# A written head, direct column transposes, and 2048-column modulation products in a hybrid decoder layer

## The chip, the cores and the metric

The kernel runs on one core of one Trainium2 chip. The metric is the device time of one execution in microseconds (us). Three runs of the kernel before took 1594.01, 1604.08 and 1601.12 us, median 1601.12.

## The reference

One layer of a decoder trunk on 256 tokens of width 2048, in float32, batch 1. What bears on this case is its start:

```python
c_act = jax.nn.silu(c)
mod = c_act @ w_mod[l] + b_mod[l]                 # 2048 -> 6 * 2048
sh1, sc1, g1, sh2, sc2, g2 = jnp.split(mod, 6, axis=-1)
h = _rms_norm(x, mix_norm_pre[l]) * (1.0 + sc1[:, None]) + sh1[:, None]
y = _token_mixer(h, ...)                          # begins with proj = h @ w_in
x = x + g1[:, None] * _rms_norm(y, mix_norm_post[l])
h = _rms_norm(x, ffn_norm_pre[l]) * (1.0 + sc2[:, None]) + sh2[:, None]
y = _conv_ffn(h, ...)                             # w_up, causal conv of width 3, silu gate, w_down
x = x + g2[:, None] * _rms_norm(y, ffn_norm_post[l])
```

The token mixer holds a sliding-window attention and a gated linear attention, whose branches are gated, added and projected. All matrices together are some 400 MB, and each is read once.

## The kernel before, in words

Every weight matrix goes through one loop over *parts* of 128x1024 (512 KB). A part is loaded into `raw` (4 buffers), split by ACT into `hi` (a cast to fp32r, L272) and by DVE into `lo` (the rest, L276; 3 buffers each), and used by TensorE three parts later. A product in this precision is three matmuls: hi x hi, lo x hi, hi x lo (L292 to L294).

*Phase 1* multiplies the scaled input by 2048 columns of `w_in` (`wS`), *phase 2* by the 2048 columns of the output gate (`wOG`). Each has 16 *items*, one for each block of 128 input channels. An item is two parts, four column blocks `n`, two token tiles `t`, so 2 x 2 x 2 x 3 = 24 matmuls of 512 columns. All eight PSUM banks accumulate over the 16 items and are emptied at the phase's end (`evac_1`, L379 and L381, and `evac_2`).

The input of item c needs modulation. Its column of `mod` is not a matmul: 128 rows of `w_mod` transposed (`wM[idx]`, 128x2048) lie on the partitions, and DVE multiplies them by `cact`, a copy of silu(c) on every partition, and sums along the row (L207). Before, this is done in two halves of 1024 columns, each in one of four buffers (`early`), and a small instruction adds both sums and the bias (L211, `modc`). In phase 1 another makes the scale `acol` (L355), then ACT writes `h` hi (L357) and DVE `h` lo (L358) from `xnT`, the transposed normalised input. In phase 2 ACT adds the shift as well (L365), casts (L297), and DVE subtracts (L298). A half whose place in the loop is q is multiplied when part q is prepared, and the buffer that it leaves is filled for a later half at once.

The *head* is all that comes before the first phase-1 matmul. It makes `cact`: DVE scales the identity by each of 16 columns of silu(c) (L136, into `t2k`), and TensorE multiplies by a matrix of ones, four matmuls of 512 columns in float32, which show as two records each (L139). ACT copies them out (L143). For each of two token tiles, DVE and ACT each square and sum one half of x (L147, L149), a power on POOL gives the reciprocal root (L115), DVE makes a diagonal of it (L120), and TensorE multiplies 16 blocks of x by that diagonal, which scales and transposes at once (L171; float32, so two records for a block). ACT copies the result to `xnT` (L173, four blocks at a time).

The order of TensorE and of the DMA queue (SP) is the order of the code. DVE and ACT follow the code inside blocks marked as manual, among them the head; elsewhere the scheduler sets their order when the program is built. All loads stand in one queue of SP, which also waits there for the buffer of a load to come free: a load that waits holds back those behind it.

Of the kernel before, what the change touches and what calls it, by code (L numbers as in the profile page):

```python
# [13 lines left out]
ALU = mybir.AluOpType  # L14
# [3 lines left out]
P = 128  # L18
# [20 lines left out]
def block_kernel(ctx: ExitStack, tc: tile.TileContext, x, cvec, pos, idn, cst, vec, vec2, gmask,  # L39
# [82 lines left out]


    cact = region("cact", [P, D], "cact")
    ones = t2k()
    nc.gpsimd.memset(ones, 1.0)
# [3 lines left out]
    with tc.manual_schedule(engines={ET.DVE, ET.Activation}):  # L130
        nc.scalar.activation(ccol, ccol, AF.Silu)

        def c_diag(n):
            dg = t2k()
            for j in range(4):
                nc.vector.tensor_scalar(out=dg[:, j * P:(j + 1) * P], in0=ident, scalar1=ccol[:, 4 * n + j:4 * n + j + 1],  # L136
                                        scalar2=None, op0=ALU.mult)
            ps = bank(n)
            nc.tensor.matmul(out=ps, lhsT=ones[:, :P], rhs=dg, start=True, stop=True)  # L139
            return ps  # L140

        def c_copy(n, ps):
            nc.scalar.copy(cact[:, n * 512:(n + 1) * 512], ps)  # L143

        def sums(t):
            ssx = small(2, "ssx")
            nc.vector.scalar_tensor_tensor(out=junk[:, t, :HW], in0=xh[:, t, :HW], scalar=1.0, in1=xh[:, t, :HW],  # L147
                                           op0=ALU.mult, op1=ALU.mult, accum_out=ssx[:, 0:1])
            nc.scalar.activation(junk[:, t, HW:], xh[:, t, HW:], AF.Square, accum_out=ssx[:, 1:2])  # L149
            return ssx  # L150

        def scale(ssx):
            ssy = small(1, "ssy")
            nc.vector.tensor_tensor(ssy, ssx[:, 0:1], ssx[:, 1:2], op=ALU.add)
            return diag_of(rstd_of(ssy, 1, float(D)))

        cps = [c_diag(n) for n in range(3)]
        c_copy(0, cps[0])
        s0 = sums(0)
        cps.append(c_diag(3))  # L160
        c_copy(1, cps[1])
        c_copy(2, cps[2])
        dgs = [scale(s0)]
        s1 = sums(1)
        c_copy(3, cps[3])
        for t in range(2):
            for q in range(4):
                pt = bank((4, 5, 6, 7, 0, 1, 2, 3)[4 * t + q])
                for j in range(4):
                    c = 4 * q + j  # L170
                    nc.tensor.matmul(out=pt[:, j * P:(j + 1) * P], lhsT=xh[:, t, c * P:(c + 1) * P], rhs=dgs[t],  # L171
                                     start=True, stop=True)
                nc.scalar.copy(xnT[:, 4 * q:4 * q + 4, t * P:(t + 1) * P], pt.rearrange("p (c t) -> p c t", c=4))  # L173
            if t == 0:
                dgs.append(scale(s1))

# [9 lines left out]
    def mod_halves(idx, post=None):  # L186
        it = {}
        return [dict(kind="mod", src=wM[idx], it=it, idx=idx, half=h, post=post) for h in range(2)]

    def bias_halves(c):  # L190
        return [dict(kind="bias", src=wS[c], c=c, half=h) for h in range(2)]
# [108 lines left out]
    def outer_mm(c, n_all, x_of, evac, split=False, mid=None):  # L300


        def one(c, t, n, hi, lo):
            xh_, xl_ = x_of()
            i = 4 * t + n
            if c == 0:
                S["acc", i] = bank(i)
            ns = slice((n % 2) * 512, (n % 2 + 1) * 512)
            ts = slice(t * P, (t + 1) * P)
            mm3(S["acc", i], xh_(c)[:, ts], xl_(c)[:, ts], hi[:, ns], lo[:, ns], c == 0, c == n_all - 1)  # L310
            if c == n_all - 1:
                evac(t, n, S["acc", i])

        def go(it, half, hi, lo):
            if not split or c < n_all - 3:
                for n in (2 * half, 2 * half + 1):
                    for t in range(2):
                        one(c, t, n, hi, lo)
                return
            for n in (2 * half, 2 * half + 1):  # L320
                one(c, 0, n, hi, lo)
            S["held", c, half] = (hi, lo)
            if c == n_all - 1 and half == 1:
# [28 lines left out]
    def make_h1(c):  # L352
        def go():
            a = acol[:, c:c + 1]
            nc.vector.scalar_tensor_tensor(out=a, in0=modc[:, 16 + c:17 + c], scalar=1.0,  # L355
                                           in1=vc[:, V_PRE1 + c:V_PRE1 + c + 1], op0=ALU.add, op1=ALU.mult)
            nc.scalar.activation(h_hi[:, c], xnT[:, c], AF.Copy, scale=a)  # L357
            nc.vector.scalar_tensor_tensor(out=h_lo[:, c], in0=xnT[:, c], scalar=a, in1=h_hi[:, c].bitcast(F32),  # L358
                                           op0=ALU.mult, op1=ALU.subtract)
        return go  # L360
# [11 lines left out]
    def evac_1(t, n, ps):  # L372
        if t == 0 and n == 0:
            S["C"] = region("C", [P, 4096], "qkv")
            S["qkv"] = S["C"][:, 0:3072].rearrange("p (t n) -> p t n", t=2)
            S["vb", 3] = vbp.tile([P, 2, 512], F32, name="vb", tag="vb")
        dst = S["vb", 3][:, t] if n == 3 else S["qkv"][:, t, n * 512:(n + 1) * 512]
        if t == 0:
            nc.scalar.copy(dst, ps)  # L379
        else:  # L380
            nc.vector.tensor_copy(dst, ps)  # L381
# [783 lines left out]
    def aux_step(q):  # L1165

        nonlocal aux_loaded, aux_done
        while aux_done < len(aux) and aux[aux_done]["pos"] <= q:
            aux_proc(aux_done)
            aux_done += 1  # L1170
        while aux_loaded < min(len(aux), aux_done + (4 if aux_done < N_EARLY - 2 else 3 if aux_done < N_PRE - 2 else 2)):
            aux_load(aux_loaded)
            aux_loaded += 1

    for q in range(n + PR):
# [9 lines left out]
        if q < n:  # L1185
# [99 lines left out]
```

## Time and profile before

| | before |
|---|---|
| runs, us | 1594.01, 1601.12, 1604.08 |
| profiled execution, us | 1597.75 |
| its span, first to last instruction, us | 1595.6 |
| TensorE busy | 1563.3 us, 98% of the span |
| VectorE (DVE) busy | 1222.5 us, 77% |
| ScalarE (ACT) busy | 825.7 us, 52% |
| bytes moved | 403.18 MB, mean 253 GB/s |
| mean granted TensorE clock | 0.997 |

The profiled execution stands 2.15 us over its span, and 3.37 us under the median of the runs. Busy time of TensorE is modelled from pipelined matmuls, so 98% says that it hardly ever waits, not that nothing could be quicker. Times within the trace are us from the span's start.

### The profile page before, as it was taken

What the parts mean: (1) busy time and instruction counts of PE and PEld (TensorE: products, weight loads), DVE (VectorE), ACT (ScalarE), POOL (GpSimd) and SP (SyncE); (2) the same over time, 40 slices, a digit from 0 to 9 for tenths busy, and PEclk for the clock granted to TensorE, in tenths of its full rate; (3) what the DMA queues carried; (4) which work ended last, traced back from release to release, by engine and by line L of the source; (5) the groups of instructions that cost most, each with busy time, mean ns of one, the idle gap of its engine ahead of it and who ended that gap; (6) DMA issues with size and microseconds to landing.
All of it is one profiled execution on the core that took longest, in us unless ns stands there. A gap on an engine that the chain in (4) does not pass through costs nothing.

```text
span 1595.6 us, 21287 instructions
## 1 busy us (share of the span) xinstructions
PE 1563.3 (98%) x7752; PEld 1293.2 (81%) x7752; DVE 1222.5 (77%) x1869; ACT 825.7 (52%) x1221; POOL 17.0 (1%) x35
## 2 busy tenths in 40 slices
PE   8999999999999999999999999999999999999997
PEld 6878888877767788777888888888778888888886
DVE  7999989968977778877778877777546777776446
ACT  5455565544477544443366555555335555555333
POOL 0000000000000000000000000000000000000001
PEclk9999999999999999999999999999999999999999
DMA  9999987877777799889935667677665555555554
GB/s 367 382 352 410 360 274 257 277 273 256 250 244 263 257 306 326 293 293 314 354 133 199 230 231 238 217 245 231 231 224 187 182 185 185 186 186 189 194 197 132
DMA packets 154841, 403.18 MB, mean 253 GB/s; under 512 B 12720, under 2 KB 70704, under 8 KB 154480
## 3 DMA queue, kind: packets, MB, share of 16 engines
q1 hardware_dynamic: 154736, 401.82, 72.9%
q8 instruction: 61, 1.00, 0.3%
q14 instruction: 44, 0.36, 0.1%
HBM read 399.68 MB, written 2.10 MB: 252 GB/s over the span
## 4 chain that ended last, share of the span: by engine, by line
PE 31%; DMA 22%; DVE 13%; issue 5%; ACT 2%; SPq 1%; POOL 0%; DVEq 0%; POOLq 0%; ACTq 0%
DMA aux<-in_wM_dram 21%; PE ps L343 16%; DVE lo L276 6%; PE ps L293 5%; PE ps L294 5%; PE ps L292 5%; DVE aux L207 2%; DMA raw<-in_wO_dram 1%; ACT hi L272 1%; SPq L251 0%; DVE aux L348 0%; DVE t2k L742 0%; DVE t2k L1093 0%; DVE y L1134 0%; SPq L253 0%
## 5 line engine op out<-in xcount | busy, mean ns | idle before, releaser
L272 ACT CAST hi<-raw 128x1024 fp32r<-128x1024 f32 x520 | 544.9, 1050 | 476.1 <-PE ps L294 366.9
L276 DVE TENSOR_TENSOR lo<-raw,hi 128x1024 fp32r<-128x1024 f32 x518 | 629.2, 1221 | 142.0 <-ACT hi L272 139.6
L343 PE MATMUL ps<-h,hi 128*128 128x512 f32 x1664 | 582.0, 398 | 1.0 <-DVE h L1051 1.0
L343 PE MATMUL ps<-h,lo 128*128 128x256 f32 x1664 | 451.0, 281 | 1.0 <-DVE lo L276 0.9
L343 PEld LDWEIGHTS ps<-h,hi 128*128 128x128 f32 x1664 | 306.4, 188 | 69.2 <-issue 1.3
L343 PEld LDWEIGHTS ps<-h,lo 128*128 128x128 f32 x1664 | 314.0, 189 | 13.8 <-DVE lo L276 4.4
L207 DVE SCALAR_TENSOR_TENSOR aux<-aux,cact 128x1024 f32<-128x1024 f32 x128 | 156.4, 1223 | 145.7 <-DMA aux<-in_wM_dram 145.6
L292 PE MATMUL ps<-hi,h 128*128 128x512 f32 x608 | 240.0, 395 | 1.6 <-ACT h L297 1.1
L293 PE MATMUL ps<-lo,h 128*128 128x512 f32 x608 | 237.4, 391 | 2.6 <-DVE lo L276 2.5
L294 PE MATMUL ps<-hi,h 128*128 128x512 f32 x608 | 237.1, 390 | 1.5 <-DVE h L298 0.8
L293 PEld LDWEIGHTS ps<-lo,h 128*128 128x128 f32 x608 | 114.2, 188 | 29.2 <-DVE lo L276 4.9
L294 PEld LDWEIGHTS ps<-hi,h 128*128 128x128 f32 x608 | 114.1, 188 | 26.9 <-DVE h L298 1.2
L292 PEld LDWEIGHTS ps<-hi,h 128*128 128x128 f32 x608 | 114.2, 188 | 26.7 <-ACT h L297 1.5
L293 PE MATMUL ps<-lo,act_ab 128*128 128x512 f32 x256 | 100.3, 392 | 2.2 <-DVE lo L276 2.2
L294 PE MATMUL ps<-hi,act_ab 128*128 128x512 f32 x256 | 99.7, 389 | 0.0
L292 PE MATMUL ps<-hi,act_ab 128*128 128x512 f32 x256 | 99.7, 389 | 0.0
L207 DVE SCALAR_TENSOR_TENSOR early<-early,cact 128x1024 f32<-128x1024 f32 x64 | 78.0, 1218 | 1.3 <-ACT cact L143 1.3
L347 ACT ACTIVATE aux<-ps 128x256 f32<-128x256 f32 x88 | 33.5, 380 | 75.4 <-PE ps L343 75.2
L1090 ACT ACTIVATE t2k<-aux,vc 128x256 f32<-128x256 f32 x88 | 52.8, 601 | 26.6 <-DVE aux L348 26.4
L348 DVE SCALAR_TENSOR_TENSOR aux<-ps,aux 128x256 f32<-128x256 f32 x88 | 37.0, 421 | 35.6 <-ACT aux L347 35.6
L293 PEld LDWEIGHTS ps<-lo,act_ab 128*128 128x128 f32 x256 | 48.0, 188 | 14.4 <-DVE lo L276 4.6
L292 PEld LDWEIGHTS ps<-hi,act_ab 128*128 128x128 f32 x256 | 48.0, 188 | 10.1
(270 smaller groups left out, 1614.2 us busy)
## 6 DMA issues: line engine op xcount, KB each, us to landing
raw<-in_wU_dram SPq DMA_DIRECT2D x176, 512.0 KB, 3.8
aux<-in_wM_dram SPq DMA_DIRECT2D x128, 512.0 KB, 6.0
raw<-in_wD_dram SPq DMA_DIRECT2D x88, 512.0 KB, 3.9
early<-in_wM_dram SPq DMA_DIRECT2D x64, 512.0 KB, 6.7
raw<-in_wS_dram SPq DMA_DIRECT2D x32, 512.0 KB, 6.4
raw<-in_wOG_dram SPq DMA_DIRECT2D x32, 512.0 KB, 7.0
aux<-in_wS_dram SPq DMA_DIRECT2D x32, 512.0 KB, 5.7
raw<-in_wQK_dram SPq DMA_DIRECT2D x32, 512.0 KB, 5.4
```

What stands on the lines that cost most here:

```text
L207: nc.vector.scalar_tensor_tensor(out=raw, in0=raw, scalar=1.0, in1=cact[:, half * HW:(half + 1) * HW], op0=ALU.mult, op1=ALU.mult, accum_o ...
L272: nc.scalar.copy(hi[:, :w], raw)
L276: nc.vector.tensor_tensor(lo[:, :w], raw, hi[:, :w].bitcast(F32), op=ALU.subtract)
L292: nc.tensor.matmul(out=o, lhsT=lh, rhs=rh, start=start, stop=False)
L293: nc.tensor.matmul(out=o, lhsT=lh, rhs=rl, start=False, stop=False)
L294: nc.tensor.matmul(out=o, lhsT=ll, rhs=rh, start=False, stop=stop)
L343: nc.tensor.matmul(out=o, lhsT=w, rhs=m, start=c == 0 and o is ps, stop=c == nk - 1 and o is ps)
L347: nc.scalar.activation(o, ps[:, TOK:], AF.Copy, scale=scale)
L348: nc.vector.scalar_tensor_tensor(out=o, in0=ps[:, :TOK], scalar=scale, in1=o, op0=ALU.mult, op1=ALU.add)
L1090: nc.scalar.activation(z, u, AF.Identity, scale=w2, bias=vc2[:, W_CB + f:W_CB + f + 1])
```

## The change

The three small loads (identity, conditioning vector, bias table) leave the SP queue for ACT's queue. The 16 diagonal scalings and the four matmuls with ones give way to 16 transposes, on TensorE, of a column of silu(c) spread over 128 columns; the fill of the ones on POOL goes. Three of the four half-squares go to DVE. For token tile 1 the diagonal goes: DVE scales x itself, in place, and TensorE transposes it in its transpose mode. The order of the head, with the first two parts' casts in it, is written out. A modulation column is one product over 2048 columns (`mod_wide`) when both halves are there; 1 + scale is folded into the bias table once, so that in phase 1 one small instruction gives `acol`. The first four matmul groups of phase 1 are reordered so that all hi x hi come first. At the end of phase 1 ACT empties two banks that DVE emptied before.

```diff
-    nc.sync.dma_start(out=ident, in_=idn)
-    nc.sync.dma_start(out=ccol, in_=cvec)
+    nc.scalar.dma_start(out=ccol, in_=cvec)
+    nc.scalar.dma_start(out=ident, in_=idn)
...
-    nc.sync.dma_start(out=vc, in_=vec)
...
+    nc.scalar.activation(ccol, ccol, AF.Silu)
+    nc.scalar.dma_start(out=vc, in_=vec)
+    for n in range(4):
+        ps = bank((2, 6, 3, 7)[n])
+        for j in range(4):
+            nc.tensor.transpose(ps[:, j * P:(j + 1) * P], ccol[:, 4 * n + j:4 * n + j + 1].to_broadcast([P, P]), ident)
+        cps.append(ps)
...
+    c_copy(0)
+    square_v(0, 0)
+    nc.scalar.activation(junk[:, 0, HW:], xh[:, 0, HW:], AF.Square, accum_out=ssx[0][:, 1:2])
+    for n in range(1, 4):
+        c_copy(n)
+    square_v(1, 0)
+    rs = rstd_x(0)
+    square_v(1, 1)
+    dg0 = diag_of(rs)
+    rs = rstd_x(1)
+    for q in range(2):
+        xs = xh[:, 1, q * HW:(q + 1) * HW]
+        nc.vector.tensor_scalar(out=xs, in0=xs, scalar1=rs, scalar2=None, op0=ALU.mult)
+    bs = vc[:, V_BMOD + 16:V_BMOD + 32]
+    nc.vector.tensor_scalar(out=bs, in0=bs, scalar1=1.0, scalar2=None, op0=ALU.add)
...
+    def mod_wide(a, raw):
+        idx = a["idx"]
+        acc = small(2, "macc")[:, 0:1]
+        nc.vector.scalar_tensor_tensor(out=raw, in0=raw, scalar=1.0, in1=cact, op0=ALU.mult, op1=ALU.mult, accum_out=acc)
+        b = vc[:, V_BMOD + idx:V_BMOD + idx + 1]
+        if idx < 16:
+            nc.vector.tensor_tensor(modc[:, idx:idx + 1], acc, b, op=ALU.add)
+        else:
+            nc.vector.scalar_tensor_tensor(out=acol[:, idx - 16:idx - 15], in0=acc, scalar=b,
+                                           in1=vc[:, V_PRE1 + idx - 16:V_PRE1 + idx - 15], op0=ALU.add, op1=ALU.mult)
+        a["post"]()
...
-        if t == 0:
+        if t == 0 or n < 2:
             nc.scalar.copy(dst, ps)
...
-        while aux_done < len(aux) and aux[aux_done]["pos"] <= q:
+        while aux_done < N_EARLY and aux[aux_done + 1]["pos"] <= q:
+            o = aux_done % 4
+            mod_wide(aux[aux_done], S["early"][:, o:o + 2].rearrange("p a k -> p (a k)"))
+            aux_done += 2
+        while N_EARLY <= aux_done < len(aux) and aux[aux_done]["pos"] <= q:
...
+            elif q == 0:
+                x_transposes(0, range(3))
+                S["lo0"] = prep(*parts[q][:2], defer=True)
+                x_transposes(0, range(3, 4))
+                x_transposes(1, range(1))
+                aux_step(1)
+                lo1 = prep(*parts[1][:2], defer=True)
+                x_transposes(1, range(1, 4))
+                lo1()
+                head.close()
+            elif q > 1:
                 prep(*parts[q][:2])
```

DVE at the head, before (`bf`: the squares, not used further; `ssx`, `ssy`, `ms`, `rs`: sums and root; `macc`: the sum of a product):

```order
L136 TENSOR_SCALAR t2k<-ident,ccol 128x128 x12
L147 SCALAR_TENSOR_TENSOR bf_116,ssx<-xh 128x1024
L136 TENSOR_SCALAR t2k<-ident,ccol 128x128 x4
L154 TENSOR_TENSOR ssy<-ssx 128x1
L113 TENSOR_SCALAR ms_156<-ssy 128x1
L120 TENSOR_SCALAR diag<-ident,rs_158 128x128
L147 SCALAR_TENSOR_TENSOR bf_116,ssx<-xh 128x1024
L207 SCALAR_TENSOR_TENSOR early,macc<-early,cact 128x1024
L154 TENSOR_TENSOR ssy<-ssx 128x1
L113 TENSOR_SCALAR ms_192<-ssy 128x1
L120 TENSOR_SCALAR diag<-ident,rs_194 128x128
```

and now:

```order
L145 SCALAR_TENSOR_TENSOR bf_113,ssx<-xh 128x1024 x2
L150 TENSOR_TENSOR ssy<-ssx 128x1
L112 TENSOR_SCALAR ms_149<-ssy 128x1
L145 SCALAR_TENSOR_TENSOR bf_113,ssx<-xh 128x1024
L119 TENSOR_SCALAR diag<-ident,rs_151 128x128
L150 TENSOR_TENSOR ssy<-ssx 128x1
L112 TENSOR_SCALAR ms_158<-ssy 128x1
L166 TENSOR_SCALAR xh<-xh,rs_160 128x1024 x2
L169 TENSOR_SCALAR vc<-vc 128x16
L199 SCALAR_TENSOR_TENSOR early,macc<-early,cact 128x2048
L204 SCALAR_TENSOR_TENSOR acol<-macc,vc 128x1
L293 TENSOR_TENSOR lo<-raw,hi 128x1024
```

The diagonal of tile 0, with which the 16 products of that tile begin, now stands behind three squares, of which the second and third need the third and fourth half of x.

SP from its loads of x on, before:

```order
L77 DMA xh<-in_x_dram 128x1024 x4
L79 DMA vc<-in_vec_dram 128x184
L239 DMA early<-in_wM_dram 128x1024 x2
L253 DMA raw<-in_wS_dram 128x1024 x2
L239 DMA early<-in_wM_dram 128x1024 x2
L253 DMA raw<-in_wS_dram 128x1024 x2
L239 DMA early<-in_wM_dram 128x1024
L253 DMA raw<-in_wS_dram 128x1024
```

and now:

```order
L77 DMA xh<-in_x_dram 128x1024 x4
L257 DMA early<-in_wM_dram 128x1024 x2
L271 DMA raw<-in_wS_dram 128x1024 x2
L257 DMA early<-in_wM_dram 128x1024 x2
L271 DMA raw<-in_wS_dram 128x1024 x2
L257 DMA early<-in_wM_dram 128x1024 x2
L271 DMA raw<-in_wS_dram 128x1024 x3
```

Where loads of modulation rows and of weights took turns one by one, they now come in pairs, since one product frees two buffers.

ACT at the end of phase 1, before (`qkv`, `vb`: the banks' contents; the first `t2k`, `h` are phase 2's first input):

```order
L379 COPY qkv<-ps_266 128x512
L272 CAST hi<-raw 128x1024
L379 COPY qkv<-ps_274 128x512
L379 COPY qkv<-ps_294 128x512
L272 CAST hi<-raw 128x1024
L379 COPY vb<-ps_302 128x512
L365 ACTIVATE t2k<-bf_116,modc,acol 128x256
L297 CAST h<-t2k 128x256
```

and now:

```order
L408 COPY qkv<-ps_252 128x512
L408 COPY qkv<-ps_254 128x512
L408 COPY qkv<-ps_256 128x512
L408 COPY qkv<-ps_258 128x512
L408 COPY qkv<-ps_281 128x512
L290 CAST hi<-raw 128x1024
L408 COPY vb<-ps_289 128x512
L394 ACTIVATE t2k<-bf_113,modc,acol 128x256
L290 CAST hi<-raw 128x1024
L315 CAST h<-t2k 128x256
```

Two more copies stand ahead, and a cast of a part has moved between the two steps of phase 2's first input. Behind phase 3's start (some 300 us) the order of every engine is the same in both.

## Rows read from the trace of the kernel before

**Rows 1.** Windows: us, busy us (count) of each engine, granted clock, DMA share, GB/s.
```profile
18.90:107.30 88.40, 87.70 (x384) 71.65 (x384) 85.98 (x144) 43.58 (x52) 0.00 (x0) 1.00 1.01 385
107.30:195.00 87.70, 85.82 (x378) 70.66 (x378) 83.37 (x130) 49.30 (x69) 0.00 (x0) 1.00 0.99 381
```

**Rows 2.** Timeline of TensorE, the head: start, us, what, [idle before <-releaser].
```profile
4.35 6.67 PE L139 MATMUL ps<-t2k 128*128 128x512 f32 x8 [4.35 <-DVE t2k L136]
10.86 7.55 PE L171 MATMUL ps<-diag,xh 128*128 128x128 f32 x64
18.91 0.50 PE L292 MATMUL ps<-hi,h 128*128 128x512 f32 x1 [0.51 <-ACT h L357]
...
20.34 0.50 PE L294 MATMUL ps<-hi,h 128*128 128x512 f32 x1 [0.69 <-DVE h L358]
```

**Rows 3.** Timeline of TensorE where phase 1 meets phase 2.
```profile
107.05 0.39 PE L294 MATMUL ps<-hi,h 128*128 128x512 f32 x1
108.51 0.50 PE L292 MATMUL ps<-hi,h 128*128 128x512 f32 x1 [1.07 <-ACT h L297]
...
110.05 0.50 PE L294 MATMUL ps<-hi,h 128*128 128x512 f32 x1 [0.81 <-DVE h L298]
```

**Rows 4.** Timeline of the SP queue at the start.
```profile
0.74 0.38 SPq L71 DMA_DIRECT2D ident<-in_idn_dram  x1
...
1.64 1.96 SPq L77 DMA_DIRECT2D xh<-in_x_dram  x4
```

**Rows 5.** The loads of tile xh (x), 0 to 11 us.
```profile
DMA to landing us min/median/max: 4.1/5.7/7.3
```

**Rows 6.** Timeline of POOL and DVE in the head.
```profile
8.73 0.55 POOL L115 TENSOR_TENSOR rs<-ms,mhalf 128x1 f32<-128x1 f32 x1 [5.83 <-DVE ms L113]
...
9.32 0.28 DVE L120 TENSOR_SCALAR diag<-ident,rs 128x128 f32<-128x128 f32 x1 [0.74 <-POOL rs L115]
```

**Rows 7.** Line L224, a DVE scaling of 1024 columns: ns min/median/max, first and last start.
```profile
L224 DVE TENSOR_SCALAR bias_v<-aux,modc x2: 747/748/748, 185.9 to 195.7; 128x1024 f32<-128x1024 f32 x2
```

**Rows 8.** Timeline of TensorE: four transposes, and what follows them.
```profile
461.42 0.60 PE L769 MATMUL ps<-ident,t2k 128*128 128x128 f32 x4
461.77 0.48 PE L292 MATMUL ps<-hi,ob 128*128 128x512 f32 x1
```

**Rows 9.** Timeline of TensorE after an idle time, in attention.
```profile
470.88 1.71 PE L783 MATMUL ps<-t2k,qkv 128*64 128x512 f32 x2 [2.38 <-ACT t2k L772]
```

**Rows 10.** Windows around it, columns as in the first group.
```profile
471.00:474.60 3.60, 3.60 (x12) 1.65 (x14) 3.16 (x6) 3.14 (x5) 0.00 (x0) 0.53 0.11 24
474.60:480.00 5.40, 5.40 (x27) 4.24 (x24) 3.90 (x13) 2.41 (x3) 0.00 (x0) 1.00 0.92 306
```

**Rows 11.** Timeline of ACT in the head.
```profile
18.33 0.54 ACT L357 ACTIVATE h<-bf,acol 128x256 fp32r<-128x256 f32 x1
...
19.64 1.05 ACT L272 CAST hi<-raw 128x1024 fp32r<-128x1024 f32 x1 [0.30 <-DMA raw<-in_wS_dram]
```

**Rows 12.** Timeline of DVE in phase 1, most of one item.
```profile
90.63 0.48 DVE L358 SCALAR_TENSOR_TENSOR h<-bf,acol,h 128x256 fp32r<-128x256 f32 x1
91.03 1.22 DVE L207 SCALAR_TENSOR_TENSOR early<-early,cact 128x1024 f32<-128x1024 f32 x1
...
92.21 1.22 DVE L276 TENSOR_TENSOR lo<-raw,hi 128x1024 fp32r<-128x1024 f32 x1
93.35 1.22 DVE L207 SCALAR_TENSOR_TENSOR early<-early,cact 128x1024 f32<-128x1024 f32 x1
...
94.61 0.22 DVE L211 SCALAR_TENSOR_TENSOR modc<-macc,vc 128x1 f32<-128x1 f32 x1
...
94.94 1.23 DVE L276 TENSOR_TENSOR lo<-raw,hi 128x1024 fp32r<-128x1024 f32 x1
```

**Rows 13.** The page's DMA issues: count, KB each, median us to landing.
```profile
early<-in_wM_dram SPq DMA_DIRECT2D x64, 512.0 KB, 6.7
```

**Rows 14.** Window of the head's second part, columns as in the first group.
```profile
8.00:20.00 12.00, 11.13 (x71) 8.58 (x69) 8.64 (x19) 9.77 (x19) 1.11 (x2) 1.00 1.03 412
```

More of the change, by code (lines that the diff above doesn't have):

```diff
@@ L124, in block_kernel @@
     cact = region("cact", [P, D], "cact")
-    ones = t2k()
-    nc.gpsimd.memset(ones, 1.0)
     bf1 = region("BF", [P, 2, KC, TOK], "bf1")
@@ L129, in block_kernel @@
     junk = bf1[:, 1].rearrange("p (t c) k -> p t (c k)", t=2)
[L130 to L134, printed above, removed]
-            for j in range(4):
[L136 to L173, printed above, removed]
-            if t == 0:
-                dgs.append(scale(s1))
@@ new lines, in block_kernel, with c_copy @@
+    head = ExitStack()
+    head.enter_context(tc.manual_schedule(engines={ET.DVE, ET.Activation}))
+    nc.scalar.activation(ccol, ccol, AF.Silu)
+    nc.scalar.dma_start(out=vc, in_=vec)
+    cps = []
+    for n in range(4):
[3 more added lines that the diff above has]
+        cps.append(ps)
+    ssx = [small(2, "ssx") for _ in range(2)]
+    def c_copy(n):
+        nc.scalar.copy(cact[:, n * 512:(n + 1) * 512], cps[n])
@@ new lines, in square_v, with rstd_x @@
+    def square_v(t, q):
+        xs = xh[:, t, q * HW:(q + 1) * HW]
+        nc.vector.scalar_tensor_tensor(out=junk[:, t, q * HW:(q + 1) * HW], in0=xs, scalar=1.0, in1=xs,
+                                       op0=ALU.mult, op1=ALU.mult, accum_out=ssx[t][:, q:q + 1])
+    def rstd_x(t):
+        ssy = small(1, "ssy")
+        nc.vector.tensor_tensor(ssy, ssx[t][:, 0:1], ssx[t][:, 1:2], op=ALU.add)
+        return rstd_of(ssy, 1, float(D))
+    c_copy(0)
+    square_v(0, 0)
+    nc.scalar.activation(junk[:, 0, HW:], xh[:, 0, HW:], AF.Square, accum_out=ssx[0][:, 1:2])
@@ new lines, in block_kernel, with x_transposes @@
+    for n in range(1, 4):
[10 more added lines that the diff above has]
+    nc.vector.tensor_scalar(out=bs, in0=bs, scalar1=1.0, scalar2=None, op0=ALU.add)
+    def x_transposes(t, qs=range(4)):
+        for q in qs:
+            pt = bank((0, 4, 1, 5, 2, 6, 3, 7)[4 * t + q])
+            for j in range(4):
+                xc = xh[:, t, (4 * q + j) * P:(4 * q + j + 1) * P]
+                if t == 0:
+                    nc.tensor.matmul(out=pt[:, j * P:(j + 1) * P], lhsT=xc, rhs=dg0, start=True, stop=True)
+                else:
+                    nc.tensor.transpose(pt[:, j * P:(j + 1) * P], xc, ident)
+            nc.scalar.copy(xnT[:, 4 * q:4 * q + 4, t * P:(t + 1) * P], pt.rearrange("p (c t) -> p c t", c=4))
@@ L188, in mod_halves @@
         return [dict(kind="mod", src=wM[idx], it=it, idx=idx, half=h, post=post) for h in range(2)]
+    def mod_wide(a, raw):
[5 more added lines that the diff above has]
+            nc.vector.tensor_tensor(modc[:, idx:idx + 1], acc, b, op=ALU.add)
+        else:
+            nc.vector.scalar_tensor_tensor(out=acol[:, idx - 16:idx - 15], in0=acc, scalar=b,
+                                           in1=vc[:, V_PRE1 + idx - 16:V_PRE1 + idx - 15], op0=ALU.add, op1=ALU.mult)
+        a["post"]()
     def bias_halves(c):
@@ L314, in go @@
         def go(it, half, hi, lo):
+            if half == 0 and c == 0 and x_of is h_of and evac is evac_1:
+                xh_, xl_ = x_of()
+                for k in range(3):
+                    for n in range(2):
+                        for t in range(2):
+                            if k == 0:
+                                S["acc", 4 * t + n] = bank(4 * t + n)
+                            nc.tensor.matmul(out=S["acc", 4 * t + n], lhsT=(xh_, xh_, xl_)[k](0)[:, t * P:(t + 1) * P],
+                                             rhs=(hi, lo, hi)[k][:, n * 512:(n + 1) * 512], start=k == 0, stop=False)
+                return
             if not split or c < n_all - 3:
@@ L354, in go @@
             a = acol[:, c:c + 1]
-            nc.vector.scalar_tensor_tensor(out=a, in0=modc[:, 16 + c:17 + c], scalar=1.0,
-                                           in1=vc[:, V_PRE1 + c:V_PRE1 + c + 1], op0=ALU.add, op1=ALU.mult)
             nc.scalar.activation(h_hi[:, c], xnT[:, c], AF.Copy, scale=a)
+            if c == 0:
+                S["lo0"]()
             nc.vector.scalar_tensor_tensor(out=h_lo[:, c], in0=xnT[:, c], scalar=a, in1=h_hi[:, c].bitcast(F32),
```

2 lines of the change are left out of this document (removed).

## The prediction

> **What bounds the kernel now.** I read the windows first, then TensorE's timeline at the places where it waits, then the engines that it waits for. In phase 1, 18.9 to 107.3 us, TensorE is busy 87.70 of 88.40 us, and in phase 2 85.82 of 87.70 [rows 1]: it waits at the head and where the phases meet, and nowhere else. DVE is nearly as full (85.98 us), and the loads run at 385 GB/s, against 412 where more is asked for [rows 1, 14]. So three resources lie close together, and TensorE ends last. The reader should see two things. Less work on DVE inside the phases buys nothing by itself. And a head that is shorter by some amount buys that amount only if DVE and the loads can follow.
>
> The stride of TensorE: phase 1 has 384 matmuls; from the third, at 20.34, to the last, at 107.05, 381 strides take 86.71 us, 0.2276 us each [rows 2, 3], an item of 24 is 5.46 us. Counted back from the third matmul by two strides, phase 1 started *in effect* at 20.34 - 0.46 = 19.9; the first one at 18.91 came before what the third needed, the low part of `h`, for which it waited 0.69 us [rows 2]. To gain, the change must bring this 19.9 down.
>
> **The head, step by step.** The 16 diagonal scalings, the four matmuls with ones and the fill on POOL go. They are hidden: the first products of tile 0 at 10.86 follow the matmuls with ones (4.35 + 6.67 = 11.02, the last one pipelined) directly [rows 2]. What replaces them, 16 transposes, is short: four take 0.60 us with the last one's tail, and 0.35 to the next matmul's start, so 0.09 to 0.15 each; I take 0.11 from here on [rows 8], and twice that at the lower clock, 3.5 us in all. They end near 7 us, long before x is there. Those three small loads cost ACT some 0.4 us each to issue, as they cost SP [rows 4]; ACT waits for the conditioning vector at that time, so nothing.
>
> The loads of x are issued first, 0.9 us earlier (0.74 instead of 1.64 [rows 4]). The last half was issued near 3.1 (three quarters into the 1.96 us of four issues) and landed at most 7.3 us later, 10.4 [rows 5]; now 9.5.
>
> DVE's written order decides what follows. The diagonal of tile 0 stands behind the square of that last half: 9.5, plus about 0.3 for the small sums ahead of it, plus 1.22 for a square (the instruction form of the product [rows 12]), plus 0.28 for the diagonal [rows 6], makes 11.3. **The products of tile 0 start at 11.3, not 10.86.** The 0.9 us of the loads is spent on moving two more squares to DVE.
>
> Then the clock. Below 11 us the records of 512 float32 columns take 6.67 / 8 = 0.83 us each, after it those of 128 columns 7.55 / 64 = 0.118 [rows 2], that is 0.47 for 512: TensorE began on the lower of its two levels, 1.2 GHz, and had the upper, 2.4 GHz, after 6.0 to 6.5 us of unbroken work. In attention it fell to the lower one (0.53 granted from 471.0 to 474.6) after an idle time of 2.38 us, and came back after 3.7 us of work from 470.88 on [rows 9, 10]. In the changed head TensorE stands idle from about 7 to 11.3, longer than those 2.38 us. So I take the lower level at 11.3, and the upper one 3.7 to 6.0 us later.
>
> The 32 records of tile 0 at 0.83 / 4 = 0.208 us: after 3.7 us 17.8 are done and 14.2 x 0.118 = 1.7 us remain, end at 16.7; after 6.0 us 28.8 are done, end at 17.7. Tile 1's 16 transposes at 0.11 add 1.8: 18.5 to 19.5. The old pair took 7.55 us [rows 2], the new one 7.2 to 8.2: the transposes save 2.0 of tile 1's 3.8 us, and the clock takes them back. Beside it runs DVE: root 0.55 [rows 6] with its two small steps to 12.3, two scalings at 0.75 [rows 7] to 13.8, the wide product to 16.1 (bounds below), 0.2 for `acol`. ACT's `h`, 0.54 [rows 11], lies beside the last transposes. So the first matmul comes at 18.5 to 19.5, and I take the middle, **19.0**. The new order inside the first item asks for the low parts only after 4 and 8 strides, when they are there, so the effective start is 19.0 too: **0.9 us gained**.
>
> A rule of the Trainium skill speaks against this head. Its page "TensorE: Matmul & The Clock Gate", section "Part 4: PE-mode transpose", says that the full clock does not engage for transposes, since they don't count as TensorE work in the same way. No row here shows it, as attention's transposes stand among matmuls. By it the sum stays as it is; without it, and with an idle time that does not matter, the result is the first rival.
>
> **The items behind it.** Item 1 now waits for DVE. From 19.0: cast of part 1 on ACT 1.05 [rows 11] to 20.05, its low part 1.15 (a DVE slot [rows 12]) to 21.2, the wide product 2.3 to 23.5, `acol` 0.2 and `h` 0.54 to 24.3. Item 1 is due at 24.5, but its low parts of weight and `h` follow at 24.9 and 25.3, due at 24.7 and 24.9: 0.4 us lost. At item 3 the scheduler's order has one more low part ahead of the product: 0.8 more, by the same sum. **1.2 us given back**; before, only 0.69 was lost here, and that is in the 19.9.
>
> **DVE per item.** Before, the two products take slots of 92.21 - 91.03 = 1.18 and 94.61 - 93.35 = 1.26, the two small ones 0.33, together 2.77 [rows 12]. The wide product, which no row shows, is at most two slots, 2.36, and hardly under 2.0, 2 x 1.22 less what one instruction may spend before its first column; I take 2.3, nearest to the slots, and 0.2 for its one small instruction. That is 0.27 less for each of 32 columns, 9 us of DVE, hidden behind TensorE: worth nothing, except that DVE catches up after item 3.
>
> **Where the phases meet.** The third matmul of phase 2 came at 110.05, due at 107.05 + 3 x 0.23 = 107.73: 2.3 us lost, to ACT's `h` first, then to DVE's low part [rows 3]. Now ACT has two copies more ahead and a cast of 1.05 between the two steps of that `h`, DVE two copies less. `h` is later by a microsecond, its low part comes at about the same time. I take 0, between -2.3 (the wait gone) and +1.
>
> **Sum.** -0.9 + 1.2 + 0 = +0.3 us against the profiled execution's 1597.75. That one lies 3.4 below the median of the runs; all four average 1599.2. So I forecast **1599 us**, no change that can be seen.
>
> **Rivals.** *The head gets shorter.* If the clock is up at 11.3, tile 0 takes 32 x 0.118 = 3.8 us, the first matmul comes at 16.9, 3.0 us under 19.9; less the 1.2, and with the phases' wait gone too, 1.8 to 4.1 us faster: 1595 to 1597. For it: the lower level at the start is read from the pace alone. Against it: the idle time. Chance 0.27.
>
> *The clock stays low through tile 1.* 11.3 + 6.7 + 16 x 0.22 = 21.5, 1.6 later than 19.9, plus the 1.2 and 1 at the meeting: up to 4 slower, 1603. Against it: the 6.0 us seen before. Chance 0.12.
>
> *Refills in pairs become the bound.* A product now frees two buffers at its end, and the product two items later needs both: 2 x 5.46 - 2.3 = 8.6 us. A load lands after 6.7 [rows 13]. With all eight buffers queued at 412 GB/s it would be 8 x 0.524 MB / 412 = 10.2 us; beyond 8.6 each pair comes late, by up to 1.6 us for two items, 32 x 0.8 = 26 us slower, 1625. For it: the loads run at 385 of 412 GB/s [rows 1, 14]. Against it: 1.9 us of slack. Chance 0.05.
>
> **How the numbers follow.** The forecast (within 1.5 us of none) has 0.56. Runs of one kernel here scatter by 5 us to each side, more than all but the last rival move. The range therefore goes from 1595 less 3 to 1603 plus 3: **1592 to 1606**. A difference under 1% (16 us) can't be told from none. Only the refill rival exceeds it, and not in all of its width: slower 0.04, faster 0.01 for what I have missed (the whole head is 19 us), same 0.95.
>
> **What would show it.** First phase-1 matmul at 18.5 to 19.5, the products of tile 0 at 11.3 on 0.21 us a record at first; waits of under 1.5 us in items 1 to 3, none afterwards; DVE busy under 80 us in phase 1; the phases' meeting within 1 us of 2.3. Wrong are a first matmul under 17.5 or over 21, a TensorE that waits in mid-phase for DVE's product behind a load, or a stride other than 0.228.

## The result, and the profile after

The changed kernel is slower: 1606.33 us median of 17 runs, where the kernel before has 1598.08 in the same series; the ratio is 1.0063, with a 95% interval of 1.0050 to 1.0077 (the two medians alone give 1.0052). One run of the kernel before, 2209.05 us, counts as slow and is not in the ratio. The profiled execution has a span of 1603.1 us against 1595.6. First the windows of the changed kernel, with the columns of [rows 1]; the engines are TensorE, its weight loads (PEld), DVE, ACT and POOL in this order. The first two windows are the two phases, the third lies in the head, the last in mid phase 1.

```profile
17.80:111.40 93.60, 91.61 (x384) 70.83 (x384) 83.94 (x98) 46.34 (x58) 0.00 (x0) 1.00 0.97 359
111.40:199.00 87.60, 85.24 (x364) 66.97 (x363) 78.45 (x93) 45.12 (x62) 0.00 (x0) 1.00 1.00 370
...
10.40:13.20 2.80, 1.39 (x12) 1.40 (x13) 1.66 (x6) 0.79 (x3) 1.58 (x2) 1.00 1.03 419
...
40.00:104.00 64.00, 62.66 (x263) 48.26 (x262) 56.56 (x67) 28.58 (x34) 0.00 (x0) 1.00 0.98 364
```

Phase 1 takes 93.6 us where it took 88.4 [rows 1]. DVE is busy for a smaller share, 83.94 of 93.60 us against 85.98 of 88.40, and the loads move 359 GB/s against 385. Two resources are less loaded, and yet TensorE is slower. That points to a chain of waits through several engines, not to a full one. TensorE's timeline has the stalls, at the head, twice in phase 1, at the phases' meeting and in phase 2:

```profile
6.72 3.65 PE L136 MATMUL ps<-ident,ccol 128*128 128x128 f32 x16 [6.72 <-DMA ident<-in_idn_dram]
11.81 3.84 PE L177 MATMUL ps<-diag,xh 128*128 128x128 f32 x32 [1.44 <-DVE diag L119]
15.48 1.91 PE L179 MATMUL ps<-ident,xh 128*128 128x128 f32 x16
17.89 1.19 PE L341 MATMUL ps<-hi,h 128*128 128x512 f32 x4 [0.49 <-ACT h L384]
...
64.85 0.39 PE L311 MATMUL ps<-lo,h 128*128 128x512 f32 x1
65.39 0.50 PE L312 MATMUL ps<-hi,h 128*128 128x512 f32 x1
...
76.57 0.40 PE L311 MATMUL ps<-lo,h 128*128 128x512 f32 x1
77.11 0.50 PE L312 MATMUL ps<-hi,h 128*128 128x512 f32 x1
...
111.28 0.39 PE L312 MATMUL ps<-hi,h 128*128 128x512 f32 x1
113.47 0.50 PE L310 MATMUL ps<-hi,h 128*128 128x512 f32 x1 [1.80 <-ACT h L315]
...
114.76 0.50 PE L312 MATMUL ps<-hi,h 128*128 128x512 f32 x1 [0.56 <-DVE h L316]
...
150.25 0.39 PE L310 MATMUL ps<-hi,h 128*128 128x512 f32 x1
150.59 0.50 PE L311 MATMUL ps<-lo,h 128*128 128x512 f32 x1
...
204.87 0.39 PE L312 MATMUL ps<-hi,h 128*128 128x512 f32 x1
```

Most stalls carry no idle mark, since one pipelined matmul covers them; the starts show them. 64.85 to 65.39 is 0.54 where 0.227 is the stride, and the same third product of the item two later stands at 77.11: two items take 77.11 - 65.39 = 11.72 us, 5.86 each, where they took 5.46. In phase 2, 150.25 to 150.59 is 0.34, a stall of 0.11. The last row is the last product of phase 2; in the kernel before it is this one:

```profile
196.55 0.39 PE L294 MATMUL ps<-hi,h 128*128 128x512 f32 x1
```

The waits from 40 to 105 us name what is late (waiting engine, awaited one: us, times, longest):

```profile
DVE lo L294 <- ACT hi L290: 7.0, 11, 0.7
...
PEld ps L312 <- DVE h L387: 6.0, 11, 0.6
...
DVE early L199 <- DMA early<-in_wM_dram: 0.6, 1, 0.6
```

From 40 to 105 us lie eleven items. In every one TensorE waits for `h` lo of DVE, and DVE for ACT's cast; for a load of `w_mod` DVE waits once.

The account against the kernel before, from the products' starts: phase 1 begins at 18.0 in effect (17.89 plus the 0.11 lost at the first one) instead of 19.9, 1.9 gained. Its last product comes at 111.28, not 107.05, so phase 1 loses 6.1. The third product of phase 2 stands 114.76 - 111.28 - 0.68 = 2.8 us late, not 2.3: 0.5 lost. Phase 2 goes from there to 204.87, 90.11 us, where it took 196.55 - 110.05 = 86.50: 3.6 lost. In all +8.3 us when phase 2 ends, and +7.5 in the span.

### The profile page after: what moved, and what is told of

Its sections match the earlier page's. It is cut to its first block, busy times and chain, and to the rows that moved or that the text cites. A ratio compares the mean times of both kernels' runs of the same rounds, so it can differ in the third digit from the quotient of the medians.

```text
span 1603.1 us, 21169 instructions
## 1 busy us (share of the span) xinstructions
PE 1563.4 (98%) x7744; PEld 1291.7 (81%) x7744; DVE 1218.2 (76%) x1775; ACT 825.6 (51%) x1221; POOL 17.4 (1%) x34
## 4 chain that ended last, share of the span: by engine, by line
PE 59%; DMA 18%; DVE 13%; issue 5%; ACT 3%; SPq 1%; POOL 0%; DVEq 0%; POOLq 0%; ACTq 0%
PE ps L372 28%; DMA aux<-in_wM_dram 16%; PE ps L312 10%; PE ps L311 10%; PE ps L310 10%; DVE lo L294 5%; DVE aux L225 1%; ACT hi L290 1%; DMA aux<-in_wS_dram 1%; DVE early L199 1%; SPq L269 1%; DMA xh<-in_x_dram 0%; DMA raw<-in_wV_dram 0%; DVE y L1163 0%; ACT aux L1031 0%
## 5 line engine op out<-in xcount | busy, mean ns | idle before, releaser
L199 DVE SCALAR_TENSOR_TENSOR early<-early,cact 128x2048 f32<-128x2048 f32 x32 | 73.1, 2286 | 1.8 <-DMA early<-in_wM_dram 1.7
```

Of the source, the lines that this page charges most:

```text
L199: nc.vector.scalar_tensor_tensor(out=raw, in0=raw, scalar=1.0, in1=cact, op0=ALU.mult, op1=ALU.mult, accum_out=acc)
```

## The theories

*T1.* The wide product is one block of 2.3 us in DVE's written order. It stands on a path from TensorE back to TensorE. In the changed kernel, DVE's rows (first phase 1, then phase 2) and ACT's:

```profile
71.83 1.23 DVE L294 TENSOR_TENSOR lo<-raw,hi 128x1024 fp32r<-128x1024 f32 x1 [0.67 <-ACT hi L290]
72.97 2.29 DVE L199 SCALAR_TENSOR_TENSOR early<-early,cact 128x2048 f32<-128x2048 f32 x1
...
75.44 1.22 DVE L294 TENSOR_TENSOR lo<-raw,hi 128x1024 fp32r<-128x1024 f32 x1
76.57 0.48 DVE L387 SCALAR_TENSOR_TENSOR h<-bf,acol,h 128x256 fp32r<-128x256 f32 x1
...
151.46 1.23 DVE L294 TENSOR_TENSOR lo<-raw,hi 128x1024 fp32r<-128x1024 f32 x1 [0.53 <-ACT hi L290]
152.60 2.28 DVE L199 SCALAR_TENSOR_TENSOR early<-early,cact 128x2048 f32<-128x2048 f32 x1
...
157.15 1.23 DVE L294 TENSOR_TENSOR lo<-raw,hi 128x1024 fp32r<-128x1024 f32 x1 [0.52 <-ACT hi L290]
```

```profile
70.75 1.05 ACT L290 CAST hi<-raw 128x1024 fp32r<-128x1024 f32 x1 [0.58 <-PE ps L312]
...
75.55 0.51 ACT L384 ACTIVATE h<-bf,acol 128x256 fp32r<-128x256 f32 x1 [0.64 <-DVE acol L204]
...
155.12 0.60 ACT L394 ACTIVATE t2k<-bf,modc,acol 128x256 f32<-128x256 f32 x1 [2.52 <-DVE modc L202]
155.76 0.41 ACT L315 CAST h<-t2k 128x256 fp32r<-128x256 f32 x1
156.07 1.04 ACT L290 CAST hi<-raw 128x1024 fp32r<-128x1024 f32 x1
```

Read phase 1 as one chain: TensorE ends an item and frees a buffer of `hi`; ACT casts into it at 70.75; DVE subtracts at 71.83, does the product at 72.97, another low part at 75.44, `h` lo at 76.57; TensorE's third product, two items after the one that freed the buffer, goes at 77.11. Between the two low parts lie 75.44 - 71.83 = 3.61 us. Before, one half stood there and the other behind `h`: 94.94 - 92.21 = 2.73 [rows 12]. The chain grew by 0.88 and went past TensorE's own time for it. In phase 2 the loop is shorter, DVE and ACT alone: low part, product, `modc`, then on ACT `t2k`, `h` and the next cast, then the next low part: 157.15 - 151.46 = 5.69 us, against the 5.44 that TensorE needs for an item.

The rivals are these. *R1*: the loads come late, because a pair of buffers comes free at once. *R2*: the shorter head leaves DVE behind from the start. *R3*: the moved evacuation copies or the first item's order cost the time. *R4*: DVE's busy share limits.

## The experiments

Ratios are to runs of the kernel before on the same chip; its medians there are 1610 to 1612 us, and only the ratios are compared. The items' times are from TensorE's starts. In the executions marked * the granted clock fell to 0.50 for 3.4 us behind the meeting of the phases, which puts the last product some 1.7 us later: compare them with 198.55, the others with 196.55. The last column comes from several chips, with one execution a row.

| | ratio, 95% interval | us an item, phase 1 | phase 2 | last product of phase 2 |
|---|---|---|---|---|
| before, as shown first | | 5.46 | 5.44 | 196.55 |
| before, again | one run | 5.46 | 5.44 | 198.55* |
| changed | 1.0063, 1.0050 to 1.0077 | 5.86 | 5.44 for four items, then 5.69 | 204.87 |
| changed, again | 1.0067, 1.0042 to 1.0092 | 5.86 | 5.44, then 5.69 | 206.41* |
| halves | 1.0012, 0.9994 to 1.0030 | 5.47 | 5.44 | 197.99* |
| halves, loads in pairs | 1.0084, 1.0054 to 1.0114 | 6.01 | 5.83 | 210.23 |
| wide half an item earlier | 1.0022, 1.0003 to 1.0040 | 5.44 | 5.69 | 201.50 |
| before with wide products | 1.0082, 1.0056 to 1.0107 | 5.86 | 5.69 | 207.14 |
| early wide, then halves | 1.0015, 1.0000 to 1.0030 | 5.44 | 5.44 | 198.15* |
| 1536 of 2048 columns | one run | 5.60 | 5.44 | 197.30 |
| five wide, then halves | 1.0005, 0.9991 to 1.0020 | 5.44 to 5.50, two at 5.8 | 5.44 | 199.62* |
| filler, early halves | 1.0007, 0.9988 to 1.0025 | 5.44 | 5.44 | 199.48* |
| filler, changed | one run | 5.86 | 5.44, then 5.69 | 205.28* |
| filler, halves | 1.0001, 0.9985 to 1.0018 | 5.47 | 5.44 | 196.77 |

**Halves in the new head.** `mod_half` is the product of one half, as in the kernel before.

```diff
...
-        while aux_done < N_EARLY and aux[aux_done + 1]["pos"] <= q:
...
-            aux_done += 2
+        while aux_done < N_EARLY and aux[aux_done]["pos"] <= q - (aux_done == 0 and q == 0):
+            mod_half(aux[aux_done], S["early"][:, aux_done % 4])
+            aux_done += 1
```

> The changed kernel with its new head, but with the modulation products of phases 1 and 2 in halves of 1024 columns at their old places and the weights loaded one half at a time. T1 (the 2.3 us product is one block in VectorE's order, and the loop it stands in, third product of an item - end of the item - cast of hi - lo - product - h_lo - third product two items later, is 11.73 us for two items against the 10.9 that TensorE needs): period of an item in phase 1 back from 5.86 to 5.45 us, last phase-1 matmul near 105.2 (before 107.05, less the head's 1.9), no 0.11 stalls in phase 2; time 1595 to 1597, that is 1 to 2 below the kernel before. R1 (pair loads come late) expects the same of this run. R2 (the shorter head leaves VectorE behind from the first item on): the period stays near 5.8 and the time near 1606.

The stalls of both phases are gone, with the new head in place: R2 falls, and so does R3, since the copies and the first item's order are those of the change. But it gains nothing on the kernel before. TensorE's timeline shows where the head's gain went:

```profile
34.67 0.39 PE L317 MATMUL ps<-hi,h 128*128 128x512 f32 x1
35.39 0.50 PE L315 MATMUL ps<-hi,h 128*128 128x512 f32 x1 [0.33 <-ACT h L389]
...
36.39 0.50 PE L317 MATMUL ps<-hi,h 128*128 128x512 f32 x1 [0.27 <-DVE h L392]
```

About 1.0 us is lost there, once, where the order takes one more low part ahead of the product: that item takes 6.53 us, its neighbours 5.55 and 5.57.

**Halves, with the loads in pairs.** To the kernel with halves is added:

```diff
+        if aux_done < N_EARLY and aux_done % 2:
+            return
         while aux_loaded < min(len(aux), aux_done + ...):
```

> As the run with halves, but SP issues the modulation weights of phases 1 and 2 only in pairs, once both halves before are used up, as the wide product makes it do. T1: the pairing costs nothing, since VectorE waited for these loads 0.6 us in all: time 1595 to 1597, period 5.45. R1 (the loads in pairs come late, VectorE or ScalarE waits for them): period near 5.8, time near 1606.

My expectation was wrong: of all versions this one ends phase 2 last, at 210.23 us. Yet DVE does not wait for a load of `w_mod` once between 40 and 104 us. Its timeline tells why: in the order that the scheduler made with loads in pairs, the two halves stand back to back. TensorE's third products follow below.

```profile
68.54 1.23 DVE L299 TENSOR_TENSOR lo<-raw,hi 128x1024 fp32r<-128x1024 f32 x1 [0.91 <-ACT hi L295]
69.68 1.22 DVE L201 SCALAR_TENSOR_TENSOR early<-early,cact 128x1024 f32<-128x1024 f32 x1
...
70.83 1.22 DVE L201 SCALAR_TENSOR_TENSOR early<-early,cact 128x1024 f32<-128x1024 f32 x1
...
72.43 1.23 DVE L299 TENSOR_TENSOR lo<-raw,hi 128x1024 fp32r<-128x1024 f32 x1
```

```profile
62.08 0.50 PE L317 MATMUL ps<-hi,h 128*128 128x512 f32 x1 [0.26 <-DVE h L392]
...
74.10 0.50 PE L317 MATMUL ps<-hi,h 128*128 128x512 f32 x1 [0.27 <-DVE h L392]
```

From low part to low part 72.43 - 68.54 = 3.89, 0.28 more than with the wide product; two items take 74.10 - 62.08 = 12.02, 0.30 more. So it is the block and not the instruction's width that costs: two halves in one place do the same harm. The run does not test R1 as I had meant it to.

**The wide product half an item earlier.**

```diff
-        while aux_done < N_EARLY and aux[aux_done + 1]["pos"] <= q:
+        while aux_done < N_EARLY and aux[aux_done + (aux_done == 0)]["pos"] <= q:
```

> The changed kernel with every wide product after the first one half-item earlier in the written order, so that its h stands ready half an item sooner. T1: the 2.3 us block leaves the stretch between the cast of an item's first half and h_lo of the same item, the 0.48 stall of each item goes, period 5.45, time 1596 to 1599. R1 (loads in pairs late) and R2 (too short a head): the load of a pair must be there half an item sooner, so it is no faster than the changed kernel: 1606 or more.

In phase 1 the order of the kinds on DVE is the same, but each product and its `h` stand one low part sooner. The stalls are gone. In its windows (phase 1, and the head) and waits:

```profile
40.00:104.00 64.00, 64.00 (x284) 53.01 (x283) 62.02 (x72) 30.97 (x37) 0.00 (x0) 1.00 1.01 397
...
13.20:16.50 3.30, 3.30 (x18) 3.30 (x18) 3.30 (x4) 1.17 (x2) 0.00 (x0) 0.50 1.03 413
```

```profile
ACT hi L290 <- DMA raw<-in_wS_dram: 14.8, 8, 2.4
```

DVE is *busier* than in the changed kernel (62.02 of 64 us against 56.56), the loads run at 397 GB/s instead of 364, still in pairs, ACT now waits for them, and TensorE does not wait at all. R1 and R4 are dead for phase 1: pairs can be fetched at this rate, and a DVE that is 97% busy does not hold TensorE up. In phase 2 I was wrong. The item stays at 5.69: where a loop closes within one item, moving all of it earlier changes nothing.

**The kernel before with wide products, and nothing else.**

```diff
...
-        while aux_done < len(aux) and aux[aux_done]["pos"] <= q:
+        while aux_done < N_EARLY and aux[aux_done + 1]["pos"] <= q:
...
```

> The kernel before with its old head, and of the change only the wide products (with the pair loads that they bring, and the 1 added once to the bias columns). T1: phase 1 goes at 5.86 us an item once VectorE's lead is used up, and phase 2 at 5.69: slower than before by 6 to 10 us, 1604 to 1608. R2 (only the shorter head makes VectorE late): as before, 1597 to 1599. R3 (the moved evacuation copies or the order of the first item cost the time): as before too, 1597 to 1599.

```profile
54.96 0.50 PE L309 MATMUL ps<-hi,h 128*128 128x512 f32 x1 [0.25 <-DVE h L371]
...
66.69 0.50 PE L309 MATMUL ps<-hi,h 128*128 128x512 f32 x1 [0.22 <-DVE h L371]
```

66.69 - 54.96 = 11.73 for two items: the same 5.86 with the old head, the old copies and the old order. The loss of the changed kernel is all here. The time went up by more than the 6 to 10 us that I had written: 13, by the interval 9 to 17. In the trace, phase 2 ends 10.6 us later than in the kernel before (207.14 against 196.55).

**Fewer columns in the product.**

```diff
-        nc.vector.scalar_tensor_tensor(out=raw, in0=raw, scalar=1.0, in1=cact, op0=ALU.mult, op1=ALU.mult, accum_out=acc)
+        nc.vector.scalar_tensor_tensor(out=raw[:, :1536], in0=raw[:, :1536], scalar=1.0, in1=cact[:, :1536],
+                                       op0=ALU.mult, op1=ALU.mult, accum_out=acc)
```

> The changed kernel as it is, with the order and the loads as they are, but each wide product multiplies only the first 1536 of its 2048 columns (the last quarter of every modulation sum of phases 1 and 2 is left out). T1: the block is 0.53 us shorter, so two items of phase 1 take 11.73 less 0.53, that is 5.60 us an item (5.86 with all columns, 5.45 without a stall), and phase 2's loop 5.69 less 0.53 falls below TensorE's pace: 5.44 with no stall. R1 (pair loads late): unchanged loads, so 5.86 and 5.69 as with all columns. R4 (it is VectorE's busy share that limits): busy falls by a tenth, no stall at all in phase 1: 5.45.

```profile
57.48 0.50 PE L313 MATMUL ps<-hi,h 128*128 128x512 f32 x1
...
79.90 0.50 PE L313 MATMUL ps<-hi,h 128*128 128x512 f32 x1
```

```profile
69.44 1.23 DVE L295 TENSOR_TENSOR lo<-raw,hi 128x1024 fp32r<-128x1024 f32 x1 [0.78 <-ACT hi L291]
70.58 1.75 DVE L199 SCALAR_TENSOR_TENSOR early<-early,cact 128x1536 f32<-128x1536 f32 x1
...
72.52 1.22 DVE L295 TENSOR_TENSOR lo<-raw,hi 128x1024 fp32r<-128x1024 f32 x1
```

Low part to low part 3.08, 0.53 less; four items in 79.90 - 57.48 = 22.42, two in 11.21, 0.51 less: 5.60 an item, the number that T1 gave and neither R1 (5.86) nor R4 (5.45) did. Phase 2's loop, 0.53 shorter, fell below TensorE's pace, and its stalls are gone, with the loads in pairs as they were: R1 falls there too. Over 3.08, 3.61 and 3.89 us of distance two items take 11.21, 11.72 and 12.02; at the 2.73 of before the same line, drawn on, would give 10.84, just less than the 10.92 that TensorE took there, and no stall showed.

**Early wide products in phase 1, halves in phase 2.**

The first loop holds the wide product, the second the halves:

```diff
...
+        while aux_done < 2 * KC and aux[aux_done + (aux_done == 0)]["pos"] <= q:
...
+        while 2 * KC <= aux_done < N_EARLY and aux[aux_done]["pos"] <= q:
...
```

> The changed kernel with the wide product of every phase-1 item half an item earlier, and in phase 2 products in halves at their old places with loads one at a time. T1 (what costs is where the 2.3 us product stands between a cast of hi and h_lo, not its busy time or its loads): period 5.44 in both phases, no stall at a third product, last phase-2 matmul 2 us ahead of the kernel before on the same chip less the clock's chance in the head; time 0 to 2 us below the kernel before, ratio 0.9985 to 1.0. R1 (pair loads) expects phase 1 at 5.8 or more: ratio 1.004.

Both phases run at TensorE's pace. The last product of phase 1 is at 105.48, against 107.47 in the kernel before on this chip. Phase 2 ends only 0.4 us ahead, though. At its second item TensorE waits again:

```profile
112.54 0.39 PE L330 MATMUL ps<-hi,h 128*128 128x512 f32 x1
114.22 0.49 PE L328 MATMUL ps<-hi,h 128*128 128x512 f32 x1 [1.29 <-ACT h L333]
115.17 0.49 PE L329 MATMUL ps<-lo,h 128*128 128x512 f32 x1 [0.46 <-DVE lo L312]
```

These are 1.68 - 0.23 us for ACT's `h` and 0.95 - 0.23 for DVE's low part, 2.2 in all: the head's 2 us were spent there. The ratio, 1.0015, lies above the 0.9985 to 1.0 that I had written.

**The kernel before and the changed one again.** 

> The kernel before, once more, for a profile on the same chip as the others. All theories: 5.45 us an item in both phases, last phase-2 matmul at 196 to 197; a difference in the rest of the program, if any, is the chip's.

> The changed kernel once more, on the chip of the others. T1: 5.86 and 5.69 us an item again, since the loop is set by fixed durations: ratio to the kernel before 1.004 to 1.008. The head's gain may differ: first phase-1 matmul at 17.9 if the full clock is granted before 11.8, up to 2 us later if it is not.

The last product of phase 2 is 7.9 us later with the change, and the ratio is the first one again. Phase 2 kept TensorE's pace up to 169 us this time, and only then fell to 5.69. In both executions the clock fell to 0.50 for 3.4 us behind the meeting of the phases (1.7 us lost in each, so 198.55 and not 197 in the kernel before), and everything after the last product of phase 2 took 1417 and 1411 us, where it had taken 1399 and 1398: that is why the times stand higher than in the first series, for both kernels.

**Five wide products, then halves.**

```diff
...
+        while aux_done < 10 and aux[aux_done + (aux_done == 0)]["pos"] <= q:
...
+        while 10 <= aux_done < N_EARLY and aux[aux_done]["pos"] <= q:
...
```

> The changed kernel with wide products half an item earlier in the first five items only, halves at their old places from the sixth on and in all of phase 2. T1: none of the stalls that halves alone had near 35 us (1.2 us in all), none in the items after them, a meeting of the phases like that of the kernel before (2.3 to 2.7 us), 5.44 us an item in both phases; last phase-2 matmul 1 to 2 us ahead of the kernel before (198.6 in its profile of this series with one fall of the clock, 196.6 without), ratio 0.9985 to 1.0005. If it is slower than that although the last phase-2 matmul is ahead, something behind phase 2 costs time that T1 does not know.

Not as expected: the extra low part comes into the order later instead, and two items near 60 us take 5.86 and 5.81, so 0.4 us is lost in each; phase 1 began late too, at 20.07. The time is that of the kernel before.

**A filler ahead of tile 0.** In the executions with the new head, tile 0's 32 records took either 3.84 us (changed, halves, early wide, 1536 columns; idle before them 1.44 to 1.70 us) or 5.4 to 5.8 (loads in pairs, wide earlier, changed again, five wide; idle 1.74 to 1.98), and the first product of phase 1 came at 17.9 to 18.3 or at 19.5 to 20.1. In the second kind the granted clock fell (wide earlier, changed again), as in the window 13.2 to 16.5 above (0.50), or the first record of it in the trace stands only at 15.4 and 16.2 us (loads in pairs, five wide), and the records of tile 0 came 0.21 us apart until then. So I gave TensorE eight more transposes to do there, in three kernels.

```diff
+    fill = bank(5)
+    for j in range(8):
+        nc.tensor.transpose(fill[:, (j % 4) * P:(j % 4 + 1) * P], ccol[:, j:j + 1].to_broadcast([P, P]), ident)
```

> The changed kernel with halves in both phases, those of phase 1 half an item earlier than at first, and eight more transposes on TensorE behind the 16 of the conditioning vector (their output is not used), so that it stands idle for less than 1 us before tile 0 instead of 1.4 to 2.0. C1 (the idle time ahead of tile 0 decides whether the full clock is there): tile 0 in 3.84 us, first phase-1 matmul at 17.9 to 18.4. C2 (chance, or transposes that do not count for the clock): tile 0 in 5.4 to 5.8 us in about half of the executions, first matmul near 20. T1 beside it: no stall in phase 1 after the first three items, last phase-2 matmul 2 us ahead of the kernel before with the same falls of the clock; ratio 0.998 to 1.000.

> The changed kernel as it is, with the eight more transposes behind the 16. C1: tile 0 in 3.84 us, first phase-1 matmul 17.9 to 18.4. C2: 5.4 to 5.8 us and 19.5 to 20 in about half of the executions. T1: phase 1 at 5.86 us an item, phase 2 at 5.69 as without them.

> The changed kernel with halves at their old places in both phases and the eight more transposes. C1: tile 0 in 3.84 us, first phase-1 matmul 17.9 to 18.4, so 1 us less than the same kernel without them on the average: ratio 0.999 to 1.001. C2: tile 0 in 5.4 to 5.8 us in half of the executions, ratio as without them, 1.001 to 1.002. T1: the stall of 1.2 us near 35 us stays.

TensorE's head in the second, the changed kernel with the filler:

```profile
10.08 1.04 PE L140 MATMUL ps<-ident,ccol 128*128 128x128 f32 x8
12.05 3.84 PE L180 MATMUL ps<-diag,xh 128*128 128x128 f32 x32 [0.93 <-DVE diag L119]
15.72 1.91 PE L182 MATMUL ps<-ident,xh 128*128 128x128 f32 x16
18.13 1.20 PE L344 MATMUL ps<-hi,h 128*128 128x512 f32 x4 [0.50 <-ACT h L387]
```

All three had tile 0 in 3.84 to 4.02 us and the first product at 18.13 to 18.43. That is what C1 expects, or close to it; under C2 three out of three would happen one time in eight, so it is supported and not settled. Two things speak against C1 as it stands. In the third kernel TensorE did not stand idle at all before tile 0, and yet the eight transposes took 1.91 us, where they took 1.04 above, and the first record of the clock stands at 12.6, behind tile 0's start. And with loads in pairs and with five wide products the clock rose late, after the same 16 transposes as elsewhere: there no fall is on the trace. When the clock rises differs from one execution to the next, and no run here shows why. The first kernel gained nothing all the same: ACT's cast stood behind an `h` that waited 5.1 us for DVE's sum, and TensorE lost 1.3 and 1.0 us at 29 to 32 us, and 0.8 in the last item of phase 1. The third has the lowest ratio: 1.0001, the time of the kernel before. No version beat it.

## Why the prediction was wrong

I forecast 1599 us, no change that can be seen; it was 1606.33 against 1598.08. Term by term: the head was -0.9 and measured -1.9; phase 1 was +1.2 and measured +6.1; the meeting was 0 and measured +0.5; phase 2 had no term and measured +3.6.

- **The step that failed** is "DVE per item": the 0.27 us saved were called "hidden behind TensorE: worth nothing, except that DVE catches up". The sum was right about the product's own length (the wide one takes 2.29, I took 2.3, and with its small one the slot is 75.44 - 72.97 = 2.47, where the four before had 2.77) and did not ask where the 2.3 us stand. Two halves had stood at two places, and only one of them between a cast and the next `h`. As one block both do. Per two items that path grew by 0.88 us, where at most 10.92 - 10.84 = 0.08 was free. It cost most of the 6.1 us in phase 1 (the last twelve items of phase 1 at 0.4 each) and, by another loop, of the 3.6 in phase 2 (eleven items at 0.25).
- **"At item 3 the scheduler's order has one more low part ahead of the product: 0.8 more"** named the very spot, and took it for a loss paid once. With halves it is (about 1 us near 35). In the changed kernel it was seen too, and items 1 to 3 together lost 1.1 us, close to the 1.2 of the sum. But with the block the order stays one low part behind to the end of the phase, and it is paid in each item; with the product half an item earlier that low part never came in, and nothing was paid. "None afterwards" was the sign that would have shown me right; there were 11 waits between 40 and 105 us. "DVE busy under 80 us in phase 1" was missed as well, at 83.94.
- **The head.** I had 19.0 and a gain of 0.9; it was 18.0 and 1.9 in the profiled execution. I had put the lower clock level into tile 0, and it ran on the upper one. The step before it failed: the transposes were to end near 7 us and leave TensorE idle to 11.3, but the identity, on ACT's queue, landed at 6.6 only; they ran from 6.72 to 10.37, and the idle time was 1.44 us. So what an idle time of 4.3 us would do was not tested. Over eight executions with this head the first product came at 17.9 to 20.1, four of each kind, so that 19.0 is near their mean (18.9) and the value of no single one. The Trainium skill's page "TensorE: Matmul & The Clock Gate", section "Part 4: PE-mode transpose", was weighed here: transposes are said not to bring the full clock. The trace disagrees. The 16 transposes take 3.65 us, 0.23 each, and nothing else had run on TensorE; the first record of the granted clock in the trace, 1.00, stands at 10.4 us, and tile 0's records then take 3.84 / 32 = 0.12 each, where they came 0.21 us apart in the executions in which the clock came late. (The windows print 1.00 ahead of the first record too; there the pace tells the level.)
- **Given back.** That a shorter head pays only as far as DVE and the loads can follow was right: with the stalls of the block taken away, the head's gain was lost again near 35 us (halves) or where the phases meet (early wide, then halves).
- **The meeting of the phases** was taken as 0 and was +0.5, inside its bounds of -2.3 and +1.
- **The rivals.** *The head gets shorter* had the clock right in half of the executions and its times wrong: the first matmul came at 17.9 at best, not at 16.9, and the block was not in it. *Refills in pairs* had the sign and the place, with another cause: loads were not what was waited for.

## What to carry to other kernels

Before two short instructions become one long one, draw the path that runs through the place where the long one will stand, from the engine that bounds back to itself, and count that path's own length per turn. An engine's busy share does not show it: here DVE was less busy, and TensorE slower. If the long form is wanted, put it a step earlier in the order, and check that the loop doesn't simply move with it.

## What the runs showed of the hardware

In eight of the eleven executions with the new head, the first record of the granted clock (1.00) stands at 9.6 to 11.4 us, when nothing but transposes had run on TensorE; in two, with the same 16 transposes, it stands at 15.4 and 16.2, and in one with the filler at 12.6. Eight further transposes took 1.04 us, 0.13 each, on the upper level (changed kernel with the filler), against 0.23 each of the sixteen.

The identity, 64 KB on ACT's queue, issued at 1.17 us, landed at 6.6, while the four loads of x, issued on SP's queue from 0.74 us on, landed at 5.0, 6.4, 8.4 and 9.6. In the kernel before it stood ahead of x on SP's queue, was issued at 0.74 and landed at 2.5. A queue of its own did not bring it in sooner; the first transposes waited for it until 6.72.
